# GpSimd, not SyncE, issues the stores of what it wrote last: the block inverses and the rotated queries and keys

## The chip, the cores and the metric

One core of a Trainium2 chip runs the whole program. The metric is device time in microseconds (us) from one launch to its end, as the median of several runs; lower is better. Engines are TensorE (PE in the profile, its weight loads PEld), VectorE (DVE), ScalarE (ACT), GpSimd (POOL) and SyncE (SP). SyncE computes nothing here: its queue issues nearly all transfers. ScalarE's queue issues the loads of the weights.

## The reference

It is one inference step of a two-layer decoder with 1024 prompt positions, 8 decode rows and a width of 1024, in float32. What matters here:

```python
p = x @ w_in                                  # q | k | v of 8 heads, and the columns of the RWKV-7 half
q, k = rope(q, pos), rope(k, pos)             # rotated; k is an output as well
att = dilated_attention_prompt(q, k, v)       # three dilated windows, 8 heads of 64
...
def step(S, inp):                             # RWKV-7 state, one position at a time
    r_t, w_t, k_t, v_t, a_t, b_t = inp
    sa = jnp.einsum('bhvk,bhk->bhv', S, a_t)
    S = S * w_t[:, :, None, :] + sa[..., None] * b_t[:, :, None, :] + v_t[..., None] * k_t[:, :, None, :]
    return S, jnp.einsum('bhvk,bhk->bhv', S, r_t)
...
x1 = layer_norm(alpha * x + concat(att, rw) @ w_out)
y = layer_norm(alpha * x1 + relu(x1 @ w_ff_up)^2 @ w_ff_down)
```

## The kernel before

The prompt is worked in two halves of 512 positions for each of the two layers. A matrix product in float32 is made as three products of split operands (lines 390 to 392), and these fill most of TensorE's time. The RWKV half is worked in units of 256 positions for a pair of heads: 2 layers x 2 halves x 4 head pairs x 2 = 32 units. The step over positions becomes chunk algebra on blocks of 64, for which a triangular matrix has to be inverted.

A unit's first stage (`stage1`) builds that matrix in the tile LB. Its 16 x 16 diagonal blocks go through HBM to 32 partitions, one block on each: SyncE stores LB to the scratch `d_el` (line 1224) and loads the blocks into BL (1227). GpSimd sets XB to the identity (1228, 1229) and inverts all 32 blocks by 15 steps of a product and a sum (1235, 1237), and then makes a transposed copy of XB, in the tile `tm` (1239). XB and the copy are stored to two more scratches (1241, 1242) and loaded from there, each in two pieces, into X and XT, with 64 rows on a partition range (1246, 1247). The second stage (`stage2`) begins with products of X (tile pT, line 1309) and XT (pX, line 1309), which double the blocks' size. XB and `tm` have one buffer each.

In `in_proj`, each of four head pairs in a half gets its q, k and v. For q and k, `rope` rotates the tile `qe`: VectorE makes the crossed product (685), GpSimd the straight product and the sum (686, 687). Four pieces of 32 partitions are stored to `d_qkv` (661), and for k the whole tile to an output (663). `att_load` loads them back, rearranged, as `stg` (1545), ScalarE and GpSimd split them (1569, 1570, 1573, 1574), and the attention begins.

GpSimd also saves the last column of a chunk of the projection for the next chunk (`lastc`, line 561; VectorE reads it at 552), mixes the first layer's values into the second's (`sg`, `z`, lines 1126 and 1129) and adds in the layer norms (738, 749).

The order of TensorE's instructions is fixed by hand: seven streams (stage 2, norm, stage 1, attention, post, cached attention, and the dense products as the filler) are interleaved by a planner (`Streams`) with costs and due times in ns. It plans a unit's second stage 30 us after its blocks were stored: `tx = R.now + 30000`. The other engines' instructions, and the order in each queue of transfers, are laid out by a scheduler that simulates the program:

```python
with tile.TileContext(nc, schedule_with_timeline_sim=True) as tc:
...
with tc.manual_schedule(engines={PE.engine}):
    R.run()
```

Each engine works its own instructions in order, and so does each queue. In the kernel before GpSimd issues no transfer at all; the program reserves 1024 bytes of each partition for the descriptors of transfers that GpSimd issues (`dynamic_dma_scratch_size=1024`, line 1899).

Of the kernel before, what the change touches and what calls it, by code (L numbers as in the profile page):

```python
# [28 lines left out]
HB = T // 2  # L29
# [118 lines left out]
class Streams:  # L148
# [27 lines left out]
    def note(self, *key):  # L176
        self.times[key] = self.now
# [90 lines left out]
def body(ctx, tc, I, O):  # L268
    nc = tc.nc
    PE, V, A, G, S = nc.tensor, nc.vector, nc.scalar, nc.gpsimd, nc.sync  # L270
# [49 lines left out]
    def both(f):  # L320
        return [[f(l, h) for h in range(2)] for l in range(DEPTH)]
# [5 lines left out]
    d_qkv = both(lambda l, h: dr.tile([4, 3, 128, HB], F32, name=f"d_qkv{l}{h}"))  # L327
# [158 lines left out]
    def rt_(name, parts=128):  # L486
        return dp.tile([parts, 532], F32, tag="r", bufs=4, name=name)
# [17 lines left out]
    def pv(l, nm, i):  # L505
        a = PROWS[nm][0] + i
        return par[l][0][:, a:a + 1]

    def pe(l, i):
        return par[l][1][:, i:i + 1]  # L510
# [29 lines left out]
    def shifted(l, h, mus, m, idx, put):  # L540

        carry = lastc[:, l, idx:idx + 1]

        def ev(it, p):
            w, _, c0, n = it
            nt = min(HB - c0, n)
            mu, omu = mus()
            u = rt_("u")
            if h == 0 and c0 == 0:
                V.memset(u[:m, 0:1], 0.0)  # L550
            else:
                V.tensor_copy(u[:m, 0:1], carry[:m])
            A.activation(u[:m, 1:1 + n], p[:m, :n], AF.Copy, scale=mu)
            d = rt_("zs")
            evs.append(V.scalar_tensor_tensor(d[:m, 0:nt], p[:m, :nt], omu, u[:m, 0:nt], op0=ALU.mult, op1=ALU.add))
            if n > nt:
                V.scalar_tensor_tensor(d[:m, nt:nt + 8], p[:m, nt:nt + 8], omu, u[:m, nt + 9:nt + 17],
                                       op0=ALU.mult, op1=ALU.add)
                nt += 8
            else:  # L560
                G.tensor_scalar(carry[:m], u[:m, nt:nt + 1], 1.0, None, op0=ALU.mult)
            put(c0, nt, d)
        return ev
# [3 lines left out]
    def sigmoid(e):  # L567

        A.activation(e, e, AF.Ln, bias=epsc[0:e.shape[0], 3:4])
        A.activation(e, e, AF.Exp, scale=-1.0)  # L570

    def in_proj(l, h, hook=None, tail=None, then=None):

        ck = CKX[h]
        dlo = d_lo[l][h]

        def put_wa(c0, n, d):
            th = rt_("th")  # L580
            G.memset(th[64:128, :n], 1.0)
            t = th[0:64, :n]
            A.activation(t, d[0:64, :n], AF.Exp, scale=2.0)
            sigmoid(t)
            G.tensor_scalar(t, t, -2.0, 1.0, op0=ALU.mult, op1=ALU.add)
            S.dma_start(dlo[0, :, c0:c0 + n], th[:, :n])
            S.dma_start(dlo[1, :, c0:c0 + n], d[:, :n])

        def put_g(c0, n, d):
            A.activation(d[:, :n], d[:, :n], AF.Exp, scale=-1.0)  # L590
            sigmoid(d[:, :n])
            S.dma_start(dlo[2, :, c0:c0 + n], d[:, :n])

        def put_v(c0, n, d):
            S.dma_start(dlo[1, 0:32, c0:c0 + n], d[0:32, :n])

        def muv(i):
            return lambda: (pv(l, "mu", i), pe(l, i))

        def z_ev(p, j):  # L600
            def put(c0, n, d):
                S.dma_start(d_z[l][h][p, j, :, c0:c0 + n], d[:, :n])
            return shifted(l, h, muv(4 * j + p), 128, 4 * j + p, put)

        lo = [(128, shifted(l, h, muv(12), 128, 12, put_wa)),
              (128, shifted(l, h, muv(13), 128, 13, put_g))]
        if l > 0:
            lo.append((32, shifted(l, h, lambda: (par[1][0][0:32, NPR:NPR + 1], par[1][1][0:32, 14:15]), 32, 14, put_v)))
        nlo = len(lo)
        lo += [(128, z_ev(0, j)) for j in range(3)]  # L610
        first = CLX[h]
        held, ends = [], list(range(len(lo)))
        for cs in ([[c] for c in first] if l > 0 else [ck]):
            end = cs[-1][0] + cs[-1][1] == HX[h]
            for i in ends[-2:] + ends[:-2] if held else ends:
                m, ev = lo[i]
                keep = not end and i in ends[-2:]
                w = held.pop(0) if held and not keep else W.take(keep)
                for c0, n in cs:
                    yield from dense([(w, m, c0, n)], K8, xhc, xlc, ev)  # L620
                if keep:
                    held.append(w)
                elif end and l > 0 and i in ends[-2:]:
                    W.release(2)
                if hook is not None and cs[0][0] == 0:
                    yield from hook(i) or ()
                if i == nlo - 1 and end:
                    note("lo", l, h)
        note("z", l, h, 0)
        tabs = ap_.tile([128, 2, HN[1]], F32, tag="tab", name="tab")  # L630
        S.dma_start(tabs, I["rope"][h])
        if tail is not None:
            tail()
        for kind, p in proj_order()[1:]:
            if kind == "a" and p == 3 and then is not None:
                yield from then()
            for j in range(3):
                w = W.take()
                if kind == "z":
                    ev = z_ev(p, j)  # L640
                    for c0, n in ck:
                        yield from dense([(w, 128, c0, n)], K8, xhc, xlc, ev)
                    continue
                seq = (2 * l + h) * 4 + p
                if j == 1 and seq > 0:
                    yield after("post", seq - 1)
                t = ap_.tile([128, HN[1]], F32, tag="qe", bufs=2, name="qe")

                def eva(it, pt):
                    _, _, c0, n = it  # L650
                    (V.tensor_copy if c0 else A.copy)(t[:, c0:c0 + n], pt[:, :n])
                for c0, n in CK[h]:
                    yield from dense([(w, 128, c0, n)], K8, xhc, xlc, eva)
                if j == 0 and h == 1:
                    t8 = ap_.tile([128, 5, 8], F32, tag="t8", name="t8")
                if j < 2:
                    rope(t, HN[h], tabs)
                    for f in range(2):
                        for d in range(2):
                            a, b = 64 * f + 32 * d, 64 * d + 32 * f  # L660
                            S.dma_start(d_qkv[l][h][p, j, b:b + 32], t[a:a + 32, 0:HB])
                    if j == 1:
                        S.dma_start(O["k_p"][l, p, :, h * HB:h * HB + HB], t[:, 0:HB])
                if h == 1 and j == 0:
                    if p == 0:
                        sq[l] = (rq.tile([128, 4, 32], F32, tag="q2", name="q2"), rq.tile([128, 4, 8], F32, tag="kn", name="kn"))
                        G.memset(sq[l][0], 0.0)
                    G.memset(t8[:, 1:4, :], 0.0)
                    for hd in range(2):
                        G.tensor_scalar(sq[l][0][:, p, hd:16:2], t[:, HB:HN[1]], C("hm")[:, hd:hd + 1], None, op0=ALU.mult)  # L670
                elif h == 1:
                    G.tensor_scalar(t8[:, (0, 4)[j - 1], :], t[:, HB:HN[1]], 1.0, None, op0=ALU.mult)
                    if j == 1:
                        G.tensor_scalar(sq[l][1][:, p, :], t[:, HB:HN[1]], 1.0, None, op0=ALU.mult)
            if kind == "a":
                qe[seq] = (l, h, p, t, t8 if h == 1 else None)
                note("qe", seq)
            note(kind, l, h, p)
# [419 lines left out]
    def dblk(d):  # L1098
        return bass.AP(tensor=d.tensor, offset=d.offset, ap=[[16 * PI + 16, 32], [PI, 16], [1, 16]])
# [6 lines left out]
    def stage1(l, h, p, u, s, lw, out):  # L1106
# [41 lines left out]
        a, f = tmp("a")[:, :n], tmp("f")[:, :n]  # L1148
# [44 lines left out]
        b = tmp("sg")[:, :n]  # L1193
# [14 lines left out]
        for cc in range(4):  # L1208
            tb, c = divmod(cc, 2)
# [11 lines left out]
        d1, d2, d3 = d_el[s % 2]  # L1221
# [4 lines left out]
        XB = tmp("XB", 256, parts=32)  # L1226
# [4 lines left out]
        for j in range(15):  # L1231
# [6 lines left out]
        XBT = tmp("tm", 256, parts=32)  # L1238
        G.tensor_scalar(XBT.rearrange("p (c t) -> p t c", c=16), XB.rearrange("p (t c) -> p t c", t=16), 1.0, None,
                        op0=ALU.mult)  # L1240
        S.dma_start(dblk(d2), XB.rearrange("p (t c) -> p t c", t=16))
        S.dma_start(dblk(d3), XBT.rearrange("p (t c) -> p t c", t=16))
        X = rp.tile([128, 4, 64], F32, tag="X", bufs=2, name="X")
        XT = rp.tile([128, 4, 64], F32, tag="XT", bufs=2, name="XT")
        for c in range(2):
# [18 lines left out]
        for cc in range(4):  # L1264
            tb, c = divmod(cc, 2)
# [648 lines left out]
```

## Time and profile before

| what | value |
|---|---|
| median of 3 runs | 3241.65 us (3232.79 to 3249.24) |
| the profiled execution | 3236.82 us |
| its span, first to last instruction | 3235.0 us |
| mean granted clock of TensorE | 0.971 |
| TensorE busy | 3055.4 us (94%) |
| VectorE, ScalarE busy | 1957.3, 1525.2 us |
| GpSimd busy | 927.0 us (29%) |

An engine's busy time is the time in which an instruction of it ran; issuing a transfer from SyncE or ScalarE is not counted as busy. Times of day are counted from the span's start.

### The profile page before, as it was taken

What the parts mean: (1) busy time and instruction counts of PE and PEld (TensorE: products, weight loads), DVE (VectorE), ACT (ScalarE), POOL (GpSimd) and SP (SyncE); (2) the same over time, 40 slices, a digit from 0 to 9 for tenths busy, and PEclk for the clock granted to TensorE, in tenths of its full rate; (3) what the DMA queues carried; (4) which work ended last, traced back from release to release, by engine and by line L of the source; (5) the groups of instructions that cost most, each with busy time, mean ns of one, the idle gap of its engine ahead of it and who ended that gap; (6) DMA issues with size and microseconds to landing.
All of it is one profiled execution on the core that took longest, in us unless ns stands there. A gap on an engine that the chain in (4) does not pass through costs nothing.

```text
span 3235.0 us, 66945 instructions
## 1 busy us (share of the span) xinstructions
PE 3055.4 (94%) x25212; PEld 2653.4 (82%) x25212; DVE 1957.3 (61%) x4471; ACT 1525.2 (47%) x3466; POOL 927.0 (29%) x1761
## 2 busy tenths in 40 slices
PE   8999999899989999989999999898999999899998
PEld 6778888777767787778899999877877777899997
DVE  4666666865565475677554466468655654964446
ACT  4445444454434364446444445345544443553444
POOL 1444435631310124453310112545242201400011
PEclk9999999999999999999999999999999999999999
DMA  7444445344343355533333236444343433422222
GB/s 229 139 134 144 131 140 152 98 127 126 104 134 105 98 158 156 156 113 105 93 90 97 90 94 182 142 138 122 108 129 107 127 120 104 136 82 92 93 91 83
DMA packets 370508, 393.65 MB, mean 122 GB/s; under 512 B 145816, under 2 KB 223080, under 8 KB 370184
## 3 DMA queue, kind: packets, MB, share of 16 engines
q10 hardware_dynamic: 121152, 213.44, 21.8%
q1 hardware_dynamic: 249032, 175.93, 19.1%
q8 instruction: 199, 3.26, 0.4%
q14 instruction: 125, 1.02, 0.1%
HBM read 325.30 MB, written 63.97 MB: 120 GB/s over the span
## 4 chain that ended last, share of the span: by engine, by line
PE 46%; DVE 6%; DMA 5%; POOL 2%; ACT 2%; issue 2%; SPq 1%; ACTq 0%; DVEq 0%; POOLq 0%
PE dps L390 13%; PE dps L391 13%; PE dps L392 12%; DVE t L760 1%; DVE t L779 1%; DMA stg<-d_qkv 1%; DVE wl L364 1%; DVE ln L748 1%; PE pX L1309 1%; DMA wr<-in_w_out 1%; POOL XB L1237 1%; PE po L1664 1%; POOL tm L1235 1%; PE pET L1641 1%; PE pS L1619 0%
## 5 line engine op out<-in xcount | busy, mean ns | idle before, releaser
L390 PE MATMUL dps<-xh,wh 128*128 128x256 f32 (+3 forms) x2984 | 975.5, 327 | 14.0 <-ACT wh L363 6.7
L391 PE MATMUL dps<-xl,wh 128*128 128x256 f32 (+3 forms) x2984 | 950.9, 319 | 9.6 <-DVE xl L782 7.5
L392 PE MATMUL dps<-xh,wl 128*128 128x256 f32 (+3 forms) x2984 | 946.1, 317 | 0.2 <-DVE u L550 0.2
L363 ACT CAST wh<-wr 128x512 fp32r<-128x512 f32 (+1 forms) x772 | 475.2, 616 | 770.2 <-PE dps L391 704.6
L364 DVE TENSOR_TENSOR wl<-wr,wh 128x512 fp32r<-128x512 f32 (+1 forms) x772 | 577.1, 748 | 406.6 <-ACT wh L363 384.6
L390 PEld LDWEIGHTS dps<-xh,wh 128*128 128x128 f32 x2984 | 570.6, 191 | 71.2 <-issue 13.6
L391 PEld LDWEIGHTS dps<-xl,wh 128*128 128x128 f32 x2984 | 570.7, 191 | 48.1 <-DVE xl L782 12.3
L392 PEld LDWEIGHTS dps<-xh,wl 128*128 128x128 f32 x2984 | 570.7, 191 | 38.2 <-DVE wl L364 0.7
L390 PE MATMUL dps<-hh,wh 128*128 128x512 f32 (+2 forms) x1600 | 525.3, 328 | 6.2 <-ACT hh L964 4.1
L391 PE MATMUL dps<-hl,wh 128*128 128x512 f32 (+2 forms) x1600 | 514.6, 322 | 4.3 <-DVE hl L965 3.5
L392 PE MATMUL dps<-hh,wl 128*128 128x512 f32 (+2 forms) x1600 | 513.5, 321 | 0.0
L390 PEld LDWEIGHTS dps<-hh,wh 128*128 128x128 f32 x1600 | 305.2, 191 | 38.3 <-issue 7.7
L391 PEld LDWEIGHTS dps<-hl,wh 128*128 128x128 f32 x1600 | 305.3, 191 | 26.9 <-DVE hl L965 4.3
L392 PEld LDWEIGHTS dps<-hh,wl 128*128 128x128 f32 x1600 | 305.0, 191 | 22.8
L1235 POOL TENSOR_TENSOR tm<-BL,XB 32x15 f32<-32x15 f32 (+7 forms) x480 | 155.4, 324 | 383.8 <-DMA BL<-d_el 295.0
L996 DVE TENSOR_TENSOR t<-dps,t 128x256 f32<-128x256 f32 (+1 forms) x240 | 123.6, 515 | 161.9 <-PE dps L392 161.4
L965 DVE TENSOR_TENSOR hl<-rl,hh 128x256 fp32r<-128x256 f32 (+2 forms) x200 | 103.4, 517 | 170.8 <-ACT hh L964 170.5
L749 POOL TENSOR_TENSOR ln<-ln,lsq 128x256 f32<-128x256 f32 (+1 forms) x112 | 93.3, 833 | 287.7 <-ACT lsq L747 285.6
L1237 POOL TENSOR_TENSOR XB<-XB,tm 32x15 f32<-32x15 f32 (+7 forms) x480 | 152.8, 318 | 33.7
L738 POOL TENSOR_TENSOR t<-t,ln 128x256 f32<-128x256 f32 (+1 forms) x32 | 28.0, 911 | 395.3 <-ACT ln L732 395.3
L738 POOL TENSOR_TENSOR t<-t,lnm 128x256 f32<-128x256 f32 (+1 forms) x80 | 69.5, 902 | 244.3 <-ACT lnm L732 230.5
L962 ACT ACTIVATE rl<-dps 128x256 f32<-128x256 f32 (+2 forms) x200 | 88.4, 442 | 94.9 <-PE dps L392 91.6
(347 smaller groups left out, 4985.9 us busy)
## 6 DMA issues: line engine op xcount, KB each, us to landing
wr<-in_w_ff_up ACTq DMA_DIRECT2D x272, 256.0 KB
wr<-in_w_ff_down ACTq DMA_DIRECT2D x256, 256.0 KB
wr<-in_w_in ACTq DMA_DIRECT2D x220, 256.0 KB
stg<-d_qkv SPq DMA_DIRECT2D x128, 128.0 KB
wr<-in_w_out ACTq DMA_DIRECT2D x64, 256.0 KB
z<-d_z SPq DMA_DIRECT2D x24, 384.0 KB
d_qkv<-qe SPq DMA_DIRECT2D x128, 64.0 KB
kvc<-in_cache_k SPq DMA_DIRECT2D x32, 256.0 KB
```

Source lines behind the costliest of these rows:

```text
L363: self.copies.append(A.copy(h[:, :, :m], w[:, :, :m]))
L364: V.tensor_tensor(lo[:, :, :m], w[:, :, :m], h.bitcast(F32)[:, :, :m], op=ALU.subtract)
L390: PE.matmul(p[:m, :n], wh[:, wk % 4, :m], hi, start=(i == 0), stop=False)
L391: PE.matmul(p[:m, :n], wh[:, wk % 4, :m], lo, start=False, stop=False)
L392: PE.matmul(p[:m, :n], wl[:, wk % 4, :m], hi, start=False, stop=(i == last))
L738: G.tensor_tensor(t, t, self.cm[:, c0:c0 + n], op=ALU.subtract)
L749: G.tensor_tensor(s2, s2, sq, op=ALU.add)
L962: A.activation(r, p[:, :n], AF.Relu)
L965: evs.append(V.tensor_tensor(hl[:, c0:c0 + n], r, hh.bitcast(F32)[:, c0:c0 + n], op=ALU.subtract))
L996: V.tensor_tensor(to, p[:, :n], to, op=ALU.add)
L1235: G.tensor_tensor(tv, bc(BL[:, 17 * j + 1:17 * j + 2], [(1, m), (0, j + 1)]), bc(XB[:, 16 * j:16 * j + 1], [(0, m), (1, j + 1)]), op=ALU.mult)
L1237: G.tensor_tensor(xv, xv, tv, op=ALU.add)
```

## The change

Three lines of calls go from SyncE's queue to GpSimd's own: the four stores of a rotated tile, the store of the rotated keys to the output, and the stores of XB and of its transposed copy. Sources, destinations and sizes stay. The loads that read the scratches back stay on SyncE, and TensorE's order stays.

```diff
@@ in_proj
                     for f in range(2):
                         for d in range(2):
                             a, b = 64 * f + 32 * d, 64 * d + 32 * f
-                            S.dma_start(d_qkv[l][h][p, j, b:b + 32], t[a:a + 32, 0:HB])
+                            G.dma_start(d_qkv[l][h][p, j, b:b + 32], t[a:a + 32, 0:HB])
                     if j == 1:
-                        S.dma_start(O["k_p"][l, p, :, h * HB:h * HB + HB], t[:, 0:HB])
+                        G.dma_start(O["k_p"][l, p, :, h * HB:h * HB + HB], t[:, 0:HB])
@@ stage1
         XBT = tmp("tm", 256, parts=32)
         G.tensor_scalar(XBT.rearrange("p (c t) -> p t c", c=16), XB.rearrange("p (t c) -> p t c", t=16), 1.0, None,
                         op0=ALU.mult)
-        S.dma_start(dblk(d2), XB.rearrange("p (t c) -> p t c", t=16))
-        S.dma_start(dblk(d3), XBT.rearrange("p (t c) -> p t c", t=16))
+        G.dma_start(dblk(d2), XB.rearrange("p (t c) -> p t c", t=16))
+        G.dma_start(dblk(d3), XBT.rearrange("p (t c) -> p t c", t=16))
```

A block store moves 32 KB as 512 pieces of 64 bytes, a store at 661 moves 64 KB as 32 rows of 2 KB, and the one at 663 moves 256 KB.

## Rows read from the trace of the kernel before

**Rows 1.** The page, busy time: us, share of the span, instructions of each engine.

```profile
PE 3055.4 (94%) x25212; PEld 2653.4 (82%) x25212; DVE 1957.3 (61%) x4471; ACT 1525.2 (47%) x3466; POOL 927.0 (29%) x1761
```

**Rows 2.** The view by stretches, first of three and their sum, columns in order.

```profile
core 0: us, PE busy (x) PEld busy (x) DVE busy (x) ACT busy (x) POOL busy (x), PEclk, DMA share, GB/s
0.00:930.00 930.00, 865.81 (x7733) 713.45 (x7734) 582.83 (x1439) 447.19 (x1061) 364.06 (x770) 0.97 0.48 139
...
sum 2030.00, PE 1898.34 PEld 1589.24 DVE 1273.44 ACT 971.94 POOL 770.11; mean PE 632.78 PEld 529.75 DVE 424.48 ACT 323.98 POOL 256.70
```

**Rows 3.** Waits of TensorE, by what ended them: us, times, longest.

```profile
PE pn L1171 <- ACT sg L570: 8.3, 6, 4.7
...
PE pT L1309 <- DMA X<-d_el: 6.9, 5, 3.7
```

**Rows 4.** Waits of SyncE's queue, by what ended them.

```profile
SPq L1241 <- POOL XB L1237: 160.6, 29, 15.4
...
SPq L661 <- POOL qe L687: 79.9, 21, 8.5
...
SPq L1246 <- DMA d_el<-XB: 30.7, 28, 2.8
```

**Rows 5.** The moved stores by line: duration of an issue in ns, min/median/max.

```profile
L1241 SPq DMA_DIRECT2D d_el<-XB x32: 302/330/531, 95.8 to 2486.7; - x32
...
L1242 SPq DMA_DIRECT2D d_el<-tm x32: 302/422/605, 97.0 to 2489.9; - x32
...
L661 SPq DMA_DIRECT2D d_qkv<-qe x128: 302/419/1152, 74.9 to 2170.7; - x128
```

**Rows 6.** The chain that ended last: start, us (of a DMA, issue to landing).

```profile
2050.80 3.13 DMA d_el<-XB
...
2054.95 0.27 SPq L1242
...
2055.56 2.48 DMA X<-d_el
...
2112.66 2.84 DMA lo<-d_lo
```

**Rows 7.** GpSimd's groups: busy us, mean ns, then the idle time before them.

```profile
L1239 POOL TENSOR_SCALAR tm<-XB 32x256 f32<-32x256 f32 x32 | 36.3, 1135 | 2.7
```

**Rows 8.** Timeline by engine, from an inverse to its use, in four units.

```profile
101.66 0.13 PEld L1309 LDWEIGHTS pT<-X,LB 64*64 64x64 f32 x1 [1.25 <-DMA X<-d_el]
...
458.02 0.33 SPq L1241 DMA_DIRECT2D d_el<-XB  x1
458.08 1.07 POOL L1239 TENSOR_SCALAR tm<-XB 32x256 f32<-32x256 f32 x1
461.48 1.27 SPq L1246 DMA_DIRECT2D X<-d_el  x2
464.63 0.30 PEld L1309 LDWEIGHTS pT<-X,LB 64*64 64x64 f32 x7 [0.17 <-issue]
...
2053.95 0.62 SPq L1246 DMA_DIRECT2D X<-d_el  x1
2056.46 0.33 PE L1309 MATMUL pT<-X,LB 64*64 64x64 f32 x2 [3.72 <-DMA X<-d_el]
...
2180.01 0.19 PEld L1309 LDWEIGHTS pT<-X,LB 64*64 64x64 f32 x2 [0.23 <-DMA X<-d_el]
```

**Rows 9.** The view by stretches, just before and just after the wait at 2056.

```profile
2048.00:2052.00 4.00, 4.00 (x35) 3.93 (x34) 2.32 (x6) 2.18 (x6) 2.31 (x6) 1.00 0.19 47
2059.70:2063.90 4.20, 4.20 (x20) 4.20 (x21) 0.42 (x1) 0.37 (x1) 0.00 (x0) 0.52 0.41 106
```

**Rows 10.** Timeline of GpSimd behind a rotation.

```profile
1232.50 1.60 POOL L687 TENSOR_TENSOR qe<-qe,rm 128x512 f32<-128x512 f32 x1
1238.08 1.56 POOL L1570 TENSOR_TENSOR qL<-stg,qS 128x512 fp32r<-128x512 f32 x1 [3.98 <-ACT qS L1569]
```

**Rows 11.** Waits of VectorE and ScalarE for GpSimd.

```profile
ACT sq L1143 <- POOL sg L1126: 35.5, 13, 5.8
...
DVE u L552 <- POOL lastc L561: 26.0, 10, 4.3
```

## The prediction, made before the result was known

> **What bounds the kernel now.** I read the page first: TensorE is busy 94% of the span, GpSimd 29% [rows 1]. So an edit to GpSimd and SyncE can help only where TensorE stands idle for them. The view by stretches says where that is: every moved store lies in 0 to 930, 1220 to 1720 or 2000 to 2600 us (elsewhere the dense feed-forward runs alone). There TensorE is busy 1898.34 of 2030 us, which leaves 131.7 us idle, and GpSimd 770.11 us, or 38% [rows 2]. The waits of TensorE come next: 131.7 us fall apart into many small groups, nearly all ended by VectorE or ScalarE; the one group ended by a transfer of this change is pT on the load of X, 6.9 us in 5 times [rows 3]. The queue of SyncE is the other side: it stands 160.6 us at line 1241 and 79.9 us at line 661 until GpSimd is done [rows 4]. The reader should see that these 240 us are waits of a queue, not of TensorE.
>
> **What the change moves.** Per unit (32 units) the stores at 1241 and 1242, per head pair (16, each for q and k) four stores at 661, and one at 663 for k: 64 + 128 + 16 = 208 issues. On SyncE one takes 0.33, 0.42 and 0.42 us [rows 5]; with 663 priced as 661 that is 32 x 0.75 + 144 x 0.42 = 84 us of queue time that SyncE loses. No row shows GpSimd issuing a transfer. Its price lies between SyncE's 0.33 us [rows 5] and, if GpSimd were held until the block has landed, 3.13 us [rows 6]. Below nothing it can't be, since the issue is an instruction that this engine did not have. I take 1.1 us: the nearest row is GpSimd's own walk over the same block of 32 x 256, the copy at 1239, 1.135 us [rows 7]. That is 208 x 1.1 = 229 us more on GpSimd, 11% of the 2030 us, and 38% becomes 49%: it does not become the bound.
>
> **Step 1, the inverses arrive later.** Before, SyncE sends XB off the moment the last product is written, 458.02 us, while GpSimd makes the transposed copy (458.08, 1.07 us); X is loaded at 461.48 and TensorE begins pT at 464.63 [rows 8]. After, the copy stands ahead of the store on the same engine: 1.14 us later, and the issue takes 1.1 instead of 0.33 us. X is 1.9 us later. In some units the store at 1242 stood between X's two loads (SyncE works at it at 2054.95, the second X goes at 2055.56 [rows 6]); without it the second load follows the first (2053.95 [rows 8]) by 0.65 us, as 1.27 us for two show in the other unit, and 0.95 us come back. Who feels it? I laid the second load of X, plus its 2.48 us [rows 6], against the first pT of each of the 32 units: the slack is under 0.2 us in four (those that begin pT at 101.66, 464.63, 2056.46 and 2180.01 [rows 8]), 3.5 to 4.9 us in five, more in 23, with a median of 9.4. For the second of the four [rows 8]: 461.48 + 0.64 + 2.48 = 464.60 against 464.63. So three units lose 1.9 us and one (at 2056.46) 0.95: 6.7 us. XT has more room, 2.4 us at the least, since pX comes after pT. A wait also costs clock: after 3.72 us without work before 2056.46 [rows 8] the granted clock is 0.52 (1.2 GHz) for 4.2 us, 20 matmuls instead of 35 in 4 us just before [rows 9]. 20 at that pace are 2.3 us, so 1.9 us were lost on about 5 us of waiting, 38% on top: **9.2 us** in all.
>
> **Step 2, GpSimd's other customers.** The rotated q and k leave as four or five issues in a row, 4.4 to 5.5 us. Behind a rotation GpSimd was idle for 3.98 us until the next work came (1232.50 + 1.60 to 1238.08) [rows 10], which hides most of it; without that cover the 32 bursts would cost 32 x 4.6 = 147 us of delay on GpSimd. Behind them wait 64 saves of the last column (lastc, line 561) for VectorE and 32 operations of the second layer's value path (sg, z) for ScalarE. Today VectorE waits 26.0 us in 10 times for the first and ScalarE 35.5 us in 13 times for the second [rows 11]. An operation meets a burst with 11% and waits half of 4.4 us: 96 x 0.11 x 2.2 = 23 us. Of ScalarE's 35.5 us TensorE felt 8.3 (pn on sg [rows 3]), so 23%: **5.4 us**. Of the heads' own use, the loads stg at 1545, the last of four stores goes 4 x (1.1 - 0.42) = 2.7 us later; the attention behind it is planned 7 to 8 us after its loads (`att_load` returns R.now + 6000 + 1000 * (h + 1)), so I price it at nothing; with no cover it would be 16 x 2.7 = 43 us.
>
> **Step 3, what SyncE gains.** Its wait at 1241 does not vanish: X's load on the same queue waits for the same store to land (30.7 us already stand there [rows 4]), so the queue is held one line further on, and longer. The 79.9 us at 661 and the 84 us of issue are truly freed, for the loads of z, lo and stg behind. Of TensorE's idle stretches I find one over 3 us that such a load ended by way of ScalarE, that of lo at 2112.66, 2.84 us [rows 6]; with the pT group's own queueing I credit **4 us**. The Trainium skill speaks against any credit (DMA: Bandwidth & Descriptors, Issuing engines are not separate DMA queues): another issuer saves only the time to issue, the transfers share the same engines. By that the sum would be 14.6 us instead of 10.6; the rows above agree in so far as the queue's waits are hardly TensorE's.
>
> **The sum** is 9.2 + 5.4 - 4 = +10.6 us on the profiled execution of 3236.82 us (span 3235.0 and 1.8 around it), 3247.4. The median of the runs shown, 3241.65, lies 4.8 us above it, so I name 3252 for a median. With GpSimd's price at 0.33 us step 1 is (3 x 1.14 + 0.19) x 1.38 = 5.0, step 2 falls with the square of the price to 0.5, and the sum is +1.5.
>
> **Rivals.** *GpSimd is the new wait.* If an issue holds it until the landing, 3.13 us, then 208 x 3.13 = 651 us make it 70% busy in the three stretches. Step 2 grows with the square (more hits, each longer): 5.4 x (3.13 / 1.1)^2 = 44 us. A burst of 12.5 us falls into a chain of some 13 us in (13 + 12.5) / 63 = 40% of the units (2030 / 32 = 63 us each): 13 units with X 6.3 us later on average; over all 32 such a delay would cost 35 us by the slacks above, so 14 us, which with step 1 (5 us) and the clock is 26. Sum 26 + 44 - 4 = +66, 3308. For it: the stores come in bursts and GpSimd runs in order. Against it: nothing in the trace says that an issue holds an engine so long; SyncE's is over in a tenth of the landing. It decides from a price of some 1.45 us, where step 1 is 11.2, step 2 is 9.4 and the sum passes 16 us. The Trainium skill has a way to get there (SBUF — State Buffer, SBUF: two separate sides): a store from GpSimd needs descriptors that its cores write through a port pair which VectorE's fast copies lock, and until then nothing moves. No run here shows it.
>
> *The freed queue pays.* Loads stood behind 160.6 + 79.9 us of waits. If z, lo and stg now go out 4 us earlier each and ScalarE's and VectorE's in-order queues close up, a sixth of the 131.7 us goes, -20 us: 3222. For it: the queue was held at 661 for 3.8 us each of 21 times. Against: so few of TensorE's waits end at a load. It decides if more than 16 us of the idle time goes.
>
> *Nothing shows.* The later X falls into slack that the order of the other engines gives anew, and the price is near SyncE's: 3242, within 5 us. Every queue except TensorE's is laid out by a scheduler from its own times (the program is built with schedule_with_timeline_sim, PE alone by hand), so the four tight units may be others or fewer; by the same road 15 us can go either way with no cause in the stores themselves.
>
> **Chances.** The forecast 0.45, with a range of its own of 3240 to 3270; nothing shows 0.18; GpSimd as the wait 0.20; the freed queue 0.12; a new order alone 0.05. About 0.5%, 16 us, is what a measurement can tell from no change. Faster: 0.12 + 0.02 = 0.14. Same: 0.33 of the forecast, 0.18, and 0.01: 0.52. Slower: 0.12 of the forecast, 0.20 and 0.02: 0.34. The range goes from the freed queue's 3222 to 3295, most of the way to the held GpSimd.
>
> **What the profile after would show.** Right: 208 new issues on GpSimd near 1.1 us each, GpSimd near 1160 us busy; SyncE's queue waiting at 1246 instead of 1241; X's loads 1 to 2 us later after the last product; TensorE's waits at pT on X some 7 us larger, with idle time in the three stretches up by 10 to 15. Wrong: an issue of 1.45 us or more, or XB's store ahead of the copy (then step 1 is a third), or groups of waits on lastc, sg and z that grow by tens of us, or loads of z and lo that end fewer waits of ScalarE (now behind SyncE) with TensorE's idle time under 115 us.

## The result, and the profile after

The changed kernel takes 3285.65 us (median of 4 runs, 3269.7 to 3295.6) against 3240.58 for the kernel before in the same session: a ratio of 1.0131, 95% interval 1.0107 to 1.0156, so 1.3% or some 43 us slower. That lies inside the range of the prediction (3222 to 3295), but 34 us above the number it named and above the forecast's own range, 3240 to 3270. Its profiled execution has a span of 3279.6 us. Wherever us of loss are given below, they are the run's ratio times the median of before in its own session.

The page, busy time [rows 1] and the new transfer queue (packets, MB, share):

```profile
PE 3054.7 (93%) x25212; PEld 2650.2 (81%) x25212; DVE 1959.7 (60%) x4471; ACT 1527.0 (47%) x3466; POOL 1041.1 (32%) x1969
...
q0 software_dynamic: 7424, 14.69, 1.7%
```

GpSimd's groups by line: busy us, mean ns of one, then the idle time ahead of them. These are the moved stores, and the copy of [rows 7]:

```profile
L661 POOL DMA_DIRECT2D d_qkv<-qe x128 | 65.6, 517 | 5.8 <-POOL qe L687 5.4
L1239 POOL TENSOR_SCALAR tm<-XB 32x256 f32<-32x256 f32 x32 | 36.5, 1141 | 2.6
L1241 POOL DMA_DIRECT2D d_el<-XB x32 | 23.3, 727 | 0.0
L1242 POOL DMA_DIRECT2D d_el<-tm x32 | 21.3, 667 | 68.1 <-issue 65.7 <-DMA z<-d_z 1.1 <-POOL ln L749 0.7
L663 POOL DMA_DIRECT2D out_k_p<-qe x16 | 9.4, 587 | 0.0
```

An issue takes 0.52 to 0.73 us, 119.6 us for all 208. Besides, GpSimd stands 68.1 us, 2.1 us a unit on average, between a block's first store and its second, for nothing that the profile names ("issue"). The stores hold it for 119.6 + 68.1 = 188 us.

Waits of TensorE [rows 3], of SyncE's queue [rows 4], and of ScalarE and VectorE for GpSimd [rows 11]: us, times, longest.

```profile
PE pT L1309 <- DMA X<-d_el: 49.6, 11, 13.9
...
SPq L1246 <- DMA d_el<-XB: 163.6, 32, 13.5
...
SPq L1545 <- DMA d_qkv<-qe: 43.6, 8, 13.0
...
ACT sq L1143 <- POOL sg L1126: 31.0, 10, 5.6
...
DVE u L552 <- POOL lastc L561: 20.4, 9, 3.5
```

The wait for pT on X has grown from 6.9 to 49.6 us [rows 3], which is nearly as much as the whole loss. SyncE's waits at 1241 and 661 are gone, and 163.6 us stand at 1246, the next line. Its loads of stg at 1545 now wait for the rope stores to land as well; in the kernel before that was

```profile
SPq L1545 <- DMA d_qkv<-qe: 6.5, 8, 3.1
```

GpSimd's two largest other customers, sg and lastc, wait a little less than before. The timeline of GpSimd in unit 26 seems to tell the story:

```profile
2187.69 0.20 POOL L1235 TENSOR_TENSOR tm<-BL,XB 32x15 f32<-32x15 f32 x1
...
2189.47 1.57 POOL L661 DMA_DIRECT2D d_qkv<-qe  x3
...
2202.61 2.07 POOL L661 DMA_DIRECT2D d_qkv<-qe  x4
2204.67 0.58 POOL L663 DMA_DIRECT2D out_k_p<-qe  x1
...
2208.44 2.00 POOL L1562 TENSOR_SCALAR qf<-stg 128x512 f32<-128x512 f32 x1 [0.92 <-PE pS L1603]
2210.40 1.99 POOL L1562 TENSOR_SCALAR kf<-stg 128x512 f32<-128x512 f32 x1
...
2222.16 0.73 POOL L1241 DMA_DIRECT2D d_el<-XB  x1
2224.79 0.67 POOL L1242 DMA_DIRECT2D d_el<-tm  x1 [1.90 <-issue]
...
2226.74 0.47 PE L1309 MATMUL pT<-X,LB 64*64 64x64 f32 x2 [13.92 <-DMA X<-d_el]
```

The chain of the inverse (1235 and 1237 in turn) runs from 2187.69 to 2221.1, and in it stand nine rope stores and the copies qf and kf. In the kernel before, the two copies came after the chain:

```profile
2174.07 1.09 POOL L1239 TENSOR_SCALAR tm<-XB 32x256 f32<-32x256 f32 x1
...
2175.59 1.99 POOL L1562 TENSOR_SCALAR qf<-stg 128x512 f32<-128x512 f32 x1 [0.17 <-PE pS L1603]
```

Behind the longer chain TensorE waits 13.92 us. In units 0, 7, 8, 18, 24 and 26 the chain takes 7 to 14 us longer than before. So theory 1 was that the issues, and what is laid around them, interrupt the chains of the inverses. Theory 2 was that the block stores cost it, theory 3 that the scheduler's new order costs it and not the issues. None of the three survived whole.

### The profile page after: what moved, and what is told of

Its sections match the earlier page's. It is cut to its first block, busy times and chain, and to the rows that moved or that the text cites. A ratio compares the mean times of both kernels' runs of the same rounds, so it can differ in the third digit from the quotient of the medians.

```text
span 3279.6 us, 67049 instructions
## 1 busy us (share of the span) xinstructions
PE 3054.7 (93%) x25212; PEld 2650.2 (81%) x25212; DVE 1959.7 (60%) x4471; ACT 1527.0 (47%) x3466; POOL 1041.1 (32%) x1969
## 5 line engine op out<-in xcount | busy, mean ns | idle before, releaser
L391 PEld LDWEIGHTS dps<-xl,wh 128*128 128x128 f32 x2984 | 568.3, 190 | 49.6 <-DVE xl L782 14.1
```

Of the source, the lines that this page charges most:

```text
L391: PE.matmul(p[:m, :n], wh[:, wk % 4, :m], lo, start=False, stop=False)
```

## The experiments

### Stores and order apart

A scheduler lays out every queue but TensorE's, and each edit moves hundreds of instructions of other engines. To hold the order still, e1 chains each engine's instructions by ordering edges, in the order of a given kernel (ORDER holds it):

```diff
     with tc.manual_schedule(engines={PE.engine}):
-        R.run()
+        R.run(); _pin(tc, nc)
+def _pin(tc, nc):
...
+        for a, b in zip(row, row[1:]):
+            tc.add_manual_dep(traced[b], traced[a].name, info, reason="pin")
```

> All 208 stores on GpSimd as in the changed kernel, but every engine keeps the order of the kernel before (ordering edges between neighbours on each engine); a head's stores stand right behind the rotation's last addition, a block's two right behind the transposing copy. So only the issues themselves differ from before. Theory 1 (the issues stand in GpSimd's order inside and just ahead of the chain of the block inverses): in the order of before the rotations fall into the chains of units 0, 3, 7, 8 and 26 and just ahead of 24; 4 to 9 issues of 0.5 us each make these chains 2 to 5 us longer, and four of them had no slack. With 1.5 to 1.9 us for copy and store, TensorE's waits at pT on X grow from 6.9 to about 30 us, and the time by about 31 us, 3272. Theory 2 (the block stores cost it): about +30 too, but spread over all tight units alike, 0, 7, 24 and 26 by the same 2 to 4 us. Theory 3 (the scheduler's new order costs it, not the issues): within 10 us of before, waits at pT under 15 us.

The edges alone, with nothing else changed, were not run. Two things in the traces speak against a cost of their own: where no store lies (the instructions of TensorE that stood at 930 to 1220 and 1720 to 2000 us), e1 and, further below, e8, e9 and e11 stay within 4 us of the time before; and in e7 (next section), which has the edges and leaves units 16 to 23 as they were, the stretch that was 1220 to 1720 takes 502.4 us instead of 499.9.

e2 has the stores of the kernel before and the order of the changed one on all engines but SyncE, e3 and e4 each do half of the diff and leave the order to the scheduler.

> The kernel before, with all stores on SyncE, but VectorE, ScalarE and GpSimd keep the order that the scheduler gave them in the changed kernel (SyncE's order is left to the scheduler). Theory 1: the new order puts other work into the chains as well (the copies qf and kf in unit 26, a second head's loads in unit 7, a rotation in unit 18), about 4 us each in units that had little slack: +5 to +15, clearly less than the whole. Theory 2: no change, within 5 us. Theory 3: most of the 45 us, 3275 or more, waits at pT of 35 us or more.

> Only the stores of the rotated queries and keys (144 of the 208 issues) go to GpSimd; the block stores stay on SyncE; the scheduler lays the engines out anew. Theory 1: most of the loss, +25 to +40 (3266 to 3281), waits at pT on X of 25 us or more in the units whose chain holds a rotation. Theory 2: under +10. Theory 3: like the changed kernel, if the new order comes from these stores; GpSimd's chains then hold other work than in the kernel before.

> Only the two stores of each block (64 issues) go to GpSimd; the scheduler lays the engines out anew. Theory 1: X is 1.2 to 1.5 us later in every unit, felt in the four without slack: +5 to +10 (3246 to 3251), waits at pT about 14 us. Theory 2 (these stores, with the second one held 2.3 us behind the first, are the cost): +25 or more. Theory 3: no forecast beyond that of theory 1; a loss of more than 15 us with chains as short as before would speak for it.

Measured, ratio to before with its interval, loss, and TensorE's wait for pT on X (6.9 us before):

| run | ratio | us | pT on X |
|---|---|---|---|
| e1, stores in the old order | 1.0173 (1.0154 to 1.0192) | +56 | 12.4 |
| e2, new order, stores on SyncE | 1.0093 (1.0077 to 1.0109) | +30 | 41.0 |
| e3, rope stores alone | 1.0058 (1.0041 to 1.0075) | +19 | 40.8 |
| e4, block stores alone | 1.0010 (0.9998 to 1.0021) | +3 | 7.8 |

The wait for X in e1, and then in e2:

```profile
PE pT L1309 <- DMA X<-d_el: 12.4, 5, 4.7
```

```profile
PE pT L1309 <- DMA X<-d_el: 41.0, 10, 12.5
```

The large wait that the profile after shows comes with the order. e2 has it without one store on GpSimd; e1, with all of them, has hardly any of it and loses more. In e1 the loss lies in small groups that VectorE and ScalarE end. One of them, unit 7, in the timelines of GpSimd, VectorE and TensorE:

```profile
410.91 1.50 POOL L1570 TENSOR_TENSOR qL<-stg,qS 128x512 fp32r<-128x512 f32 x1
412.49 0.45 POOL L1574 TENSOR_TENSOR kS<-stg,kS 64x128 fp32r<-64x128 f32 x1
...
414.79 0.21 POOL L561 TENSOR_SCALAR lastc<-u 128x1 f32<-128x1 f32 x1
...
415.04 0.15 DVE L552 COPY u<-lastc 128x1 f32<-128x1 f32 x1 [7.01 <-POOL lastc L561]
...
415.87 0.27 DVE L1396 TENSOR_SCALAR Z<-pO,Wd 128x64 f32<-128x64 f32 x1
...
416.19 0.48 PE L1389 MATMUL pO<-Z,FG 64*64 64x64 f32 x4 [4.87 <-DVE Z L1396]
```

A one-column save on GpSimd is late; VectorE, which works in order too, stands 7.01 us for it; the product Z that is queued behind it is late, and TensorE stands 4.87 us, put down to VectorE. The waits for GpSimd in e1, and then in e9 (below):

```profile
DVE u L552 <- POOL lastc L561: 44.3, 12, 9.2
...
ACT sq L1143 <- POOL sg L1126: 51.0, 13, 7.6
...
ACT sg L1140 <- POOL z L1129: 15.5, 6, 4.9
```

```profile
DVE u L552 <- POOL lastc L561: 52.4, 12, 11.1
...
ACT sq L1143 <- POOL sg L1126: 54.2, 15, 8.5
...
ACT sg L1140 <- POOL z L1129: 20.9, 7, 4.8
```

lastc and sg were 26.0 and 35.5 us [rows 11], so 18 and 16 us more in e1. z, before:

```profile
ACT sg L1140 <- POOL z L1129: 9.1, 6, 3.1
```

Theory 2 falls with e4. Theory 3 has the order right and leaves e1's 56 us unexplained.

### Is the interrupted chain the cause?

e6 puts whatever stood inside six chains of the changed kernel behind them, e7 does so with five chains of the kernel before. The edit is to ORDER alone, as a sketch:

```diff
-  chain ops, foreign ops between them, 1239, 1241, 1242
+  chain ops, 1239, 1241, 1242, foreign ops
```

> The changed kernel with every engine in its order there, except that in units 0, 7, 8, 18, 24 and 26 all foreign work of GpSimd that stood inside the chain of the inverse (124 instructions, rope stores among them) stands behind the chain's second store. Theory 1 (X is late because the chains are interrupted): these chains fall to 11 to 13 us, the waits at pT on X from 49.6 to under 10, and the time by 30 us or more, to 3255 or less. Theory 3 in a stricter form (GpSimd has more in these stretches than fits, whatever stands first): the waits at pT go, but kS, lastc, z and the others are 10 to 15 us later in these units, TensorE waits for VectorE and ScalarE instead, and the time stays within 15 us of the changed kernel or rises.

> The kernel before, all stores on SyncE, every engine in its order there, except that in units 0, 7, 8, 24 and 26 GpSimd's foreign work (58 instructions) stands behind the chain. It takes 5 to 12 us out of five chains. Theory 1: the four tight units get slack, the 6.9 us at pT go: -5 to -10 us, and it would beat both kernels a little. Stricter theory 3: there was no loss at X to win back, and what is put behind the chain is late: +10 to +30.

e6: 1.0269 (1.0251 to 1.0288), +87 us; e7: 1.0082 (1.0066 to 1.0099), +27. The waits for pT on X go down to 19.0 and 5.3 us, and the time goes up. Waits of VectorE and TensorE in e6:

```profile
DVE rt L700 <- POOL qe L687: 27.3, 2, 14.2
DVE rm L685 <- POOL qe L687: 24.2, 2, 14.4
```

```profile
PE pT L1309 <- DMA X<-d_el: 19.0, 8, 5.6
...
PE pqt L698 <- ACT qe L651: 14.9, 1, 14.9
...
PE dps L390 <- DVE u L552: 12.3, 1, 12.3
```

The two groups for qe aren't in the kernel before at all. What was put behind the chain is now waited for. Theory 1 falls in its form "free the chain and the loss is gone". The late X comes with the new order (e2) and can be traded for other waits (e6), so it is where a loss comes out and not by itself its source. Both runs put all foreign work behind the chain; putting back only what the new order had let in was not tried.

### GpSimd's time by itself

e8 and e11 split e1: the rope stores and the block stores alone, each in the old order. e9 moves no store at all and adds copies that nobody reads, at the places where e1 has the stores.

```diff
-        G.tensor_tensor(t[:, :n], t[:, :n], m[:, :n], op=ALU.add)
+        _pad(nc, dur, cst[0:32, 0:64], held, G.tensor_tensor(t[:, :n], t[:, :n], m[:, :n], op=ALU.add), 7)
...
-        G.tensor_scalar(XBT.rearrange("p (c t) -> p t c", c=16), XB.rearrange("p (t c) -> p t c", t=16), 1.0, None,
-                        op0=ALU.mult)
+        _pad(nc, dum, cst[0:32, 0:128], held, G.tensor_scalar(XBT.rearrange("p (c t) -> p t c", c=16), XB.rearrange("p (t c) -> p t c", t=16), 1.0, None,
+                        op0=ALU.mult), 6)
```

> As e1 (every engine in the order of the kernel before), but only the stores of the rotated queries and keys go to GpSimd; the block stores stay on SyncE in their places. e1 lost 56 us with both. If GpSimd's time alone counts, the rope stores hold it for 75 of 186 us, so +22. If it counts where they stand (in bursts of 4 to 9 inside the chains and ahead of lastc, z and sg), most of the 56 is theirs, +40 or more, and the block stores are worth 5 to 15.

> As e1 and e8 (every engine in the order of the kernel before), with only the block stores on GpSimd. e1 lost 56 us with all stores, e8 23 with the rope stores. If GpSimd's time adds up, +25 to +35 here, and the scheduler's new order is what brought e4 back to +3. If the two kinds of stores hurt each other, +5 to +12 here.

> The kernel before, every store on SyncE, every engine in its order there, plus work of GpSimd that nobody uses (it is added to the computation, nothing is left out): behind each rotation seven small copies of 32x64, behind each transposing copy of XB six of 32x128, at the places where the changed kernel's stores stand in e1; by the 1.14 us of the copy of 32x256 about 2.2 and 3.6 us, 187 us in all, against 182 to 186 us that the stores hold GpSimd. If what costs is GpSimd's time in its fixed order, whatever fills it: +45 to +60, as e1, with lastc and sg late as there. If it is the stores' own path (the landing, the later load of X behind copy and issue, the queue of SyncE at 1246): within 15 us of before.

GpSimd's added groups in e9 (line 1918 is the helper that adds them), and then the moved stores in e1:

```profile
L1918 POOL TENSOR_SCALAR dum<-cst 32x128 f32<-32x128 f32 x192 | 135.9, 708 | 13.2
L1918 POOL TENSOR_SCALAR dur<-cst 32x64 f32<-32x64 f32 x224 | 116.1, 518 | 15.9
```

```profile
L661 POOL DMA_DIRECT2D d_qkv<-qe x128 | 65.3, 515 | 9.7 <-POOL qe L687 9.7
...
L1241 POOL DMA_DIRECT2D d_el<-XB x32 | 23.3, 729 | 0.0
L1242 POOL DMA_DIRECT2D d_el<-tm x32 | 21.2, 662 | 67.0 <-issue 67.0
L663 POOL DMA_DIRECT2D out_k_p<-qe x16 | 9.3, 582 | 0.0
```

The idle copies came out at 252 us instead of the 187 that were meant: the small ones cost far more per element than the copy of 32x256.

| run, old order | GpSimd held, us (issues + hold) | ratio | loss, us | loss per us held |
|---|---|---|---|---|
| e8, rope stores | 75 | 1.0070 (1.0051 to 1.0088) | 23 | 0.30 |
| e11, block stores | 44 + 66 | 1.0116 (1.0098 to 1.0134) | 38 | 0.34 |
| e1, both | 119 + 67 | 1.0173 | 56 | 0.30 |
| e9, idle copies, no store moved | 252 | 1.0190 (1.0173 to 1.0208) | 62 | 0.25 |

Each loss is uncertain by some 6 us. e8 and e11 add up to 61, e1 has 56. The waits for lastc, sg and z in the same runs, in us:

| run | lastc | sg | z | sum above before | loss |
|---|---|---|---|---|---|
| before | 26.0 | 35.5 | 9.1 | | |
| e8 | 35.0 | 42.1 | 7.3 | 14 | 23 |
| e11 | 38.8 | 46.8 | 15.1 | 30 | 38 |
| e1 | 44.3 | 51.0 | 15.5 | 40 | 56 |
| e9 | 52.4 | 54.2 | 20.9 | 57 | 62 |

Idle copies at the same places lose time in the same way as the stores, with the same waits. So in a fixed order it is in the main GpSimd's time that costs, whatever fills it: 0.25 to 0.34 us of the kernel for each us. At the 0.25 of e9 the stores of e1 would cost 46 us (186 x 0.25, an estimate); the 10 us above that may be the stores' own path, and lie at the edge of the uncertainty.

### The hold ahead of the second store

e5 is the changed kernel with one number changed, e10 is e4 with the same:

```diff
-    nc = bacc.Bacc("TRN2", target_bir_lowering=False, num_devices=1, dynamic_dma_scratch_size=1024)
+    nc = bacc.Bacc("TRN2", target_bir_lowering=False, num_devices=1, dynamic_dma_scratch_size=1536)
```

> The changed kernel with one number changed: GpSimd's descriptor memory is 1536 instead of 1024 bytes (dynamic_dma_scratch_size). Every engine's order stays that of the changed kernel. Two block stores of 512 pieces should then fit at once, and the 68 us that GpSimd stands ahead of the second one (2.1 us in each unit) should go. If the time that GpSimd is held counts wherever it falls, about half of its extra 182 us (114 busy, 68 held) is gone and the loss goes from 45 to 25 us or less. If what counts is what stands in the chains of the inverses ahead of the first store, nothing changes: within 8 us of the changed kernel, waits at pT on X still 45 to 50 us. If the hold is not the descriptor memory's, the idle time ahead of the second store stays at 60 to 70 us.

> As e4 (only the block stores on GpSimd, same order of every engine as there), with 1536 instead of 1024 bytes of descriptor memory, so that the second store isn't held for 2 us. e4 was within 0.2% of before with 64 us of such idle time. If GpSimd's held time costs 0.25 to 0.3 us of the kernel per us, as e5 against the changed kernel says, this gives 15 to 19 us back and the kernel beats both, 3228 to 3235 on the scale of 3245 for before. If in e4's order that time lies in GpSimd's idle stretches: no change against e4, within 5 us.

The second store in e4, in e5 and in e10:

```profile
L1242 POOL DMA_DIRECT2D d_el<-tm x32 | 21.3, 666 | 65.1 <-issue 64.0 <-POOL ln L749 0.7 <-POOL kS L1574 0.4
```

```profile
L1242 POOL DMA_DIRECT2D d_el<-tm x32 | 21.4, 667 | 0.0
```

```profile
L1242 POOL DMA_DIRECT2D d_el<-tm x32 | 21.2, 663 | 0.0
```

The 68 and 65 us are gone with every engine's order unchanged. e5: 1.0073 (1.0054 to 1.0091), +24 instead of +43, so 19 us for 68. e10: 0.9951 (0.9936 to 0.9966), -16 instead of e4's +3, so 19 us for 65. That is 0.28 and 0.29 us per us held, now in two orders that the scheduler made; the two differences are uncertain by some 10 and 6 us. e10 beats both kernels, by 0.5% and 1.8%. In time e5 did what was expected if held time counts wherever it falls; its waits for pT on X still sum to 46.5 us, so most of the gain lies in other waits.

What ends the hold can be read from the changed kernel's trace, in the timelines of GpSimd and of SyncE's queue in units 4 and 26:

```profile
279.64 0.75 POOL L1241 DMA_DIRECT2D d_el<-XB  x1
283.66 0.61 SPq L1246 DMA_DIRECT2D X<-d_el  x1
284.10 0.67 POOL L1242 DMA_DIRECT2D d_el<-tm  x1 [3.71 <-issue]
...
2222.16 0.73 POOL L1241 DMA_DIRECT2D d_el<-XB  x1
2224.37 1.27 SPq L1246 DMA_DIRECT2D X<-d_el  x2
2224.79 0.67 POOL L1242 DMA_DIRECT2D d_el<-tm  x1 [1.90 <-issue]
```

SyncE loads X as soon as the first store has landed (all 32 waits at 1246 are for it). From one store's end to the next one's start it is 1.75 to 4.14 us, but the second store starts 0.29 to 0.44 us after SyncE's load in every one of the 32 units. So with 1024 bytes GpSimd stands until the first block has landed. What holds it, the program or the engine, the runs don't show.

### The other direction

```diff
-        G.tensor_scalar(XBT.rearrange("p (c t) -> p t c", c=16), XB.rearrange("p (t c) -> p t c", t=16), 1.0, None,
-                        op0=ALU.mult)
+        A.copy(XBT.rearrange("p (c t) -> p t c", c=16),
+               XB.rearrange("p (t c) -> p t c", t=16))
```

> The other direction: the kernel before, all stores on SyncE, but the transposing copy of XB (36 us of GpSimd in all) is made by ScalarE; the scheduler lays the engines out anew. If GpSimd's time costs 0.25 to 0.3 us per us, -9 to -11, and it beats both kernels, 3234 to 3237 on the scale of 3245; ScalarE's queue then waits for XB in some units and may take some of it back. If the kernel before has GpSimd's work covered where it stands: within 5 us. A new order alone can move it by 20 us either way, as e2 showed.

0.9989 (0.9977 to 1.0001), -4 us: no more than the measurement can tell, and less than the 9 to 11 expected. GpSimd is busy 887.6 us instead of 927.0, but ScalarE waits 62.6 us in 23 times for XB, which it didn't before, and the order is new. The run is inconclusive: it can't tell a gain that ScalarE took back from no gain.

## Why the prediction was right and wrong

The time fell within the range by the range's width and not by the steps: its upper part was there for a rival with a chance of 0.20. The sum had the sign right, but +10.6 us is a quarter of the 43, and "slower" had 0.34 against 0.52 for "same". By its steps:

**What bounds the kernel.** "38% becomes 49%: it does not become the bound" was the wrong way to ask. GpSimd was busy 43% of the same three stretches [rows 2]:

```profile
sum 2030.00, PE 1861.95 PEld 1561.88 DVE 1251.38 ACT 961.54 POOL 879.66; mean PE 620.65 PEld 520.63 DVE 417.13 ACT 320.51 POOL 293.22
```

With the hold of 68.1 us that is 47%, less than forecast, and yet every us that it was held cost 0.25 to 0.34 us where the order was kept. VectorE and ScalarE work in order and wait for single small results of it, so its average idle time can't be spent.

**The price.** 1.1 us for an issue was too high, 0.57 us came (119.6 / 208). What no step had is the hold ahead of each second block store, 2.1 us on average, until the first has landed. With it the stores hold GpSimd for 188 us instead of 229, so the total was not the fault. An issue by itself does end long before its block has landed, as the forecast assumed. The Trainium skill (Perfetto Trace Analysis, DMA Instruction — SWDGE (GPSIMD)) says what the row then is: the end of an issue from GpSimd in a profile is the last descriptor written. The trace agrees in so far as the row ends early: in unit 26 it lasts 0.73 us, and X's load, released by the landing, starts 2.21 us after it began.

**Step 1, X later,** was sized at 9.2 us. The order copy, store came as described, and XB's store starts 1.0 us later after the last product. X's second load then starts 4.4 us after the last product instead of 3.2 (medians of the 32 units): 1.3 us later, where 1.9 were forecast. But block stores alone move TensorE's wait on X from 6.9 to 7.8 us (e4) or 8.3 (e11), since the tight units did not stay tight. In e11 units 0 and 8, which began pT at 101.66 and 464.63 [rows 8], come to pT 10.1 and 8.5 us after the last product, instead of 5.9 and 6.6, and don't wait for X at all: TensorE was held up elsewhere before. Nor did the clock's 38% come as forecast. In the changed kernel TensorE is idle 45 us longer and busy no longer than before (3054.7 us, mean granted clock 0.970, against 3055.4 and 0.971); in e1 it is idle 50 us longer and busy 11.5 us longer (0.966), in e9 58 and 18 (0.963).

**Step 2, the other customers,** is the step that failed. It forecast 23 us of waits for lastc, sg and z and took 23% of them as TensorE's, 5.4. In e1 these waits grew by 40 us and the kernel lost 56; for the rope stores alone it was 14 and 23 (e8), for the block stores alone 30 and 38 (e11). So the waits came at less than twice the forecast, but the kernel lost 1.1 to 1.7 us for each us of them (e9 included) and not 0.23: one of ScalarE's waits for sg as TensorE felt it had been carried over to everything that stands behind GpSimd. These three waits are not the whole path. ScalarE's waits for stg at qS and kS, which had been priced at nothing, grew by 9.5 us each in e1 (24.7 to 34.2, 39.8 to 49.3) and by 6 each in e8 (to 31.0 and 45.7). How much of each wait TensorE felt wasn't separated. And some 60% of the loss in the old order came from the block stores, for which the step that the prediction worked out, X's path, is worth 1.4 us in TensorE's wait (6.9 to 8.3).

**Step 3** had the wait's move from 1241 to 1246 right. It was wrong that the 79.9 us at 661 are freed: the loads of stg on the same queue now wait for the rope stores to land, 43.6 us at 1545 instead of 6.5. Its credit of 4 us can't be seen in the old order, where moving stores off SyncE (e1, 56 us) cost about what the same places filled with idle copies do (e9, 62 us, for more time held).

**The rivals.** "GpSimd is the new wait" was given 0.20 and came nearest. Its condition, that an issue holds GpSimd until the landing, held for 32 of the 208, the second block stores that stand until the first has landed. It put its turning point at 1.45 us an issue; it came at 0.57 with the hold, 0.90 us a store. Its picture of bursts within the chains is what the trace after shows, and e6 speaks for a place and not a cause. "A new order alone" was sized at 15 us either way and got 0.05; e2 measures 30 us for it. In the changed kernel the parts don't add: 30 for its order without the stores, and 13 more with them, while the same stores cost 56 in the old order. Why the stores cost less in the order that the scheduler made with them in it isn't shown.

What stays open: why the scheduler's order for the block stores is so much better than the old one. e4 and e11 have the same stores and the same descriptor memory, and e4 stands at +3, e11 at +38. Whether these 35 us come of SyncE's freed queue, which the scheduler may use and a fixed order may not, or of its order by chance, wasn't tried; e4's order with the stores on SyncE would tell.

## What to carry to other kernels

Price work added to an engine that others wait for in order by the time it holds that engine, including time in which it stands at its own issue, at a rate measured by filling the same places with idle work; the engine's busy share says little. Where a scheduler lays out the queues, the wait that grows in the profile shows where the order let the shortage out: hold the order still, and run the order without the edit, before naming a cause. Look for idle time ahead of an issue that nothing in the profile ends; here one constant removed it and turned the block stores' half of the change into a gain (e10).

## What was not expected of the hardware

- An issue from GpSimd took 0.52 us for 32 rows of 2 KB, 0.59 us for 128 rows of 2 KB and 0.67 to 0.73 us for a block of 32 KB, which lies in HBM as 512 pieces of 64 bytes. The profile counts 528 packets for such a store on SyncE's queue and 32 on GpSimd's (e4 has 33792 packets fewer on q1 than the kernel before, and 2048 on q0, for 64 stores), so a price per piece can't be read from it.
- GpSimd stood ahead of a second block store until the first had landed, 2.1 us on average, with 1024 bytes of descriptor memory, and not at all with 1536 (e5, e10). Four or five rope stores in a row were not held. The Trainium skill (DMA: Bandwidth & Descriptors, Terms) has a descriptor at 16 bytes, written to rings in SBUF. By that, an estimate, 512 pieces with a descriptor each, spread evenly over rings for 16 engines, take 32 x 16 = 512 bytes of each ring before anything is added to end the store, and two such stores just don't fit into 1024 bytes and do into 1536. The runs show the two sizes alone, and neither the rings nor the number of descriptors.
- Copies on GpSimd took 0.52 us for 32x64 and 0.71 us for 32x128 elements, behind 1.14 us for 32x256 of the same kind: a quarter of the elements for nearly half of the time.
